# A two-layer decoder trunk on one core: the first expert pair in two halves, a norm's rows by transfer, gathers that skip empty slots, and buffers handed to the weight stream in another order

## The chip, the cores and the metric

The kernel runs on one core of a Trainium2 chip. Its time is device microseconds of one execution. The engines are TensorE (PE; its weight loads are listed apart as PEld), VectorE (DVE), ScalarE (ACT), GpSimd (POOL) and SyncE (SP). SP computes nothing here: it issues the weight transfers one after the other. ACT and POOL issue transfers too.

## The reference, cut to what matters

256 tokens of 1024 features go through two layers. Each layer mixes tokens (layer A by a gated linear recurrence, layer B by stick-breaking attention, both with four heads of attention into a fixed memory), projects the result, adds it to the input and normalises; then a mixture of experts follows, with a second add and norm.

```python
x = post_norm(x, mixed @ w_o[layer], ln_mix_g[layer], ln_mix_b[layer])
moe_out = hier_moe(x, w_group[layer], b_group[layer], w_router[layer], b_router[layer],
                   w_gate[layer], w_up[layer], w_down[layer])
x = post_norm(x, moe_out, ln_ffn_g[layer], ln_ffn_b[layer])
...
# hier_moe: top-1 of 4 groups, then top-2 of its 4 experts; 16 experts of 256 inner features
h = jax.nn.silu(jnp.einsum('td,edf->tef', xf, w_gate)) * jnp.einsum('td,edf->tef', xf, w_up)
y = jnp.einsum('tef,efd->td', h * gates[:, :, None].astype(h.dtype), w_down)
```

## The kernel before, in words

**Experts by pairs.** Each token goes to 2 of 16 experts. An expert has 64 slots (`CAP`), and two experts make a pair of 128 slots, one per partition. So there are 8 pairs, 1024 slots, and 512 of them hold a token when none overflows; the rest are empty. In `Moe.run` a pair p goes through these steps: `gu` multiplies its 128 rows by the gate and up weights (8 blocks `kk` of 128 features, two experts `c` side by side in two column halves of PE, 512 output columns: 256 of gate, 256 of up); ACT takes silu of the gate half and DVE multiplies by the up half and the slot's weight (`h`, lines 873 and 875); PE transposes `h` (`ht`, line 899), ACT copies it to `hT` (line 900), PE multiplies by the down weights (`po`, line 913) in two halves of 512 columns. A matmul of the program on float32 shows as two records in the trace. In pairs 1 to 7, blocks of the next pair's `gu` stand between these steps, so that PE has work while ACT and DVE finish. Pair 0 has no such work in between: `gu(0)`, `turn(1)` (two small matmuls `ptp`), two `ht`, then `po`. Pair 0's `h` is already cut into two column halves for ACT and DVE, but both halves of gate and up lie in one PSUM bank, and all of `gu(0)` ends first.

**Rows of a pair.** Pair 0's rows are made by matmuls with a one-hot matrix. For pairs 1 to 7 the normalised tokens `z` are stored to a buffer `zd` in HBM and gathered into one of two row tiles `zg` (POOL, `fetch`, line 673) by an index per slot; PE then transposes the rows (`xgp`, line 791), and ACT and DVE apply the norm's gain and bias per feature. The index of an empty slot is 256, and a gather leaves out indices above 255. `zg` is not cleared, so for pairs 1 and 2, the first ones into each tile, line 665 takes the index down to at most 255: their empty slots fetch row 255. The later gathers leave empty slots out. Output rows of pairs 0 to 4 are scattered to a buffer `hd` (line 760) and brought back per token near the end (line 752); pairs 5 to 7 are combined by matmuls into `y`.

**The weight stream.** All weights are 133 chunks of 1 MB in the order of use. `Stream` issues them on SP, in a fixed order, and at most three are under way (`DEPTH`: a chunk is issued when the third before it has landed). A chunk goes to a free buffer: nine in a ring `w`, and other tiles that are free for a while (`x0`, `x1`, `m0`, `m1`, `wa` to `wd`, `o0`, `gb`), which `stream.open` hands over. `late` chunks, the first two of each layer's experts, go to the tiles `u` and `ex` by `stream.send`. Each pair takes six chunks: two for `kk` 0 to 3 (one per expert), two for `kk` 4 to 7, two for `po`. Layer A's experts are chunks 23 to 70, layer B's 85 to 132. A chunk that waits for its buffer holds back every chunk behind it on SP.

**Norm rows.** `rows` brings gain and bias of a norm into the tile `gb`: one row by transfer, and two broadcasts over the partitions on POOL (line 384); for the last norm the transfer itself writes all 128 partitions (line 380). `affine` applies them to the tokens on DVE (lines 438 and 440), token half 0 after `gu(0)`, half 1 behind pair 0's `h`. Then `gb` is opened for weights.

**Order.** Inside the two mixer ends DVE, PE and ACT keep the written order, and so does what `pin` marks; the rest is placed by a scheduler that simulates the program. So the changed source does not by itself tell the order of instructions.

Of the kernel before, what the change touches and what calls it, by code (L numbers as in the profile page):

```python
# [15 lines left out]
P = 128  # L16
D = 1024
# [25 lines left out]
def trunk(ctx: ExitStack, tc: tile.TileContext, w_all, x_tok_d, cst_d, msk_d, rw_d, rb_d,  # L43
# [331 lines left out]

    def rows(which, name, by_transfer=False):

        gb = tok_tile("gb", f"gb{name}")
        if by_transfer:
            nc.scalar.dma_start(gb, ln_d[0, 2 * which:2 * which + 2].partition_broadcast(P))  # L380
            return gb
        nc.scalar.dma_start(gb[0:1], ln_d[:, 2 * which:2 * which + 2])
        for v in range(2):
            ins = nc.gpsimd.partition_broadcast(gb[:, v], gb[0:1, v])  # L384
            if which % 2:
                tc.keep_in_program_order(ins)
        return gb

    class Norm:
# [39 lines left out]
        def apply(self, dst, src):  # L429
            nc.scalar.activation(dst, src, AF.Identity, scale=self.r, bias=self.nmr)  # L430

# [111 lines left out]
    class Moe:  # L543
# [87 lines left out]
        def start(self, pool):  # L631
            self.work = pool
            self.zg = slots.tile([P, 2, D], F32, tag="o1", name=f"zg{self.l}")

        def gather_first(self, z, t):

            l = self.l
            P0 = self.P0[:, t].rearrange("p e c -> p (e c)")
            if t == 0:
                self.first = [bank(f"xgp{l}", tag="y", shape=(P, 4, P)) for _ in range(2)]  # L640
            for hk in range(2):
                for k in range(4):
                    kk = 4 * hk + k
                    nc.tensor.matmul(self.first[hk][:, k], z[:, t, kk * P:(kk + 1) * P], P0, start=(t == 0 and k == 0),
                                     stop=(t == 1 and k == 3), skip_group_check=True)
# [7 lines left out]
        def indices(self):  # L653

            l = self.l
            self.P1f = self.P1.rearrange("p t e c -> p t (e c)")
            self.idx = self.rt("idx", (8,), I32)
            ps = bank(f"idx{l}", tag="m", shape=(P, 8))
            for p in range(8):
                for t in range(NT):  # L660
                    nc.tensor.matmul(ps[:, p:p + 1], self.P1f[:, t, p * P:(p + 1) * P], tokb[:, t:t + 1], start=(t == 0),
                                     stop=(t == 1))


            pin(nc.vector.tensor_scalar(self.idx[:, 0:3], ps[:, 0:3], float(T), T - 1.0, op0=ALU.add, op1=ALU.min))
            for p in (1, 2):
                self.fetch(p)
            self.filled = self.rt("filled", (8,))
            nc.vector.tensor_scalar(self.idx[:, 3:8], ps[:, 3:8], float(T), None, op0=ALU.add)
            nc.vector.tensor_copy(self.filled, ps)  # L670
# [132 lines left out]
        def run(self, xg):  # L803
# [7 lines left out]

            def gu(p, ks):

                if p not in ws:
                    ws[p] = [stream.get() for _ in range(6)]
                    gus[p] = bank(f"gu{l}", tag="y" if p <= AWAY else "m")
                for kk in ks:
                    kh, k = kk // 4, kk % 4
                    for c in range(2):
                        pin(nc.tensor.matmul(gus[p][c * 64:(c + 1) * 64], xgs[p][:, kk, c * CAP:(c + 1) * CAP],  # L820
                                            ws[p][2 * kh + c][0][:, k * 512:(k + 1) * 512], start=(kk == 0),
                                            stop=(kk == NK - 1)))
                    if k == 3:
                        stream.done(ws[p][2 * kh][1], ws[p][2 * kh + 1][1])
# [11 lines left out]
            for p in range(8):  # L836
                if p == 0:
                    gu(0, range(4))
                    self.gates()
                    self.turn(0)  # L840
                    gu(0, range(4, 8))
                    self.ex = slots.tile([P, 2, D], F32, tag="ex", name=f"ex{l}")
# [28 lines left out]
                parts = [slice(0, 256)] if p else [slice(0, P), slice(P, 256)]  # L871
                for c in parts:
                    nc.scalar.activation(h[:, c], gus[p][:, c], AF.Silu)  # L873
                for c in parts:
                    pin(nc.vector.scalar_tensor_tensor(h[:, c], gus[p][:, 256 + c.start:256 + c.stop],
                                                       self.gsl[:, p:p + 1], h[:, c], op0=ALU.mult, op1=ALU.mult))
                if p == 0:
# [14 lines left out]
                if p == 7:  # L892
                    beyond(pool, self.pool, self.ex, l, base, self.x1, self.most, self.late, y)
                hT = pool.tile([P, 2, P], F32, name=f"hT{l}")
                for c in parts:
                    fs = slice(c.start // P, c.stop // P)
                    ht = bank(f"ht{l}", tag="m", shape=(P, 2, P))
                    for f in range(fs.start, fs.stop):
                        pin(nc.tensor.transpose(ht[:, f], h[:, f * P:(f + 1) * P], ident))  # L899
                    nc.scalar.activation(hT[:, fs], ht[:, fs], AF.Copy)  # L900
                if 0 < p < 7:
                    gu(p + 1, range(2, 3))
# [5 lines left out]
                for hf, s in enumerate(half if p < 7 else quarters):  # L908
                    n = s.stop - s.start
                    po = bank(f"po{l}", tag="m")[:, 0:n]  # L910
                    for f in range(2):
                        for c in range(2):
                            pin(nc.tensor.matmul(po[c * 64:(c + 1) * 64], hT[:, f, c * 64:(c + 1) * 64],  # L913
                                                ws[p][4 + c][0][:, f * D + s.start:f * D + s.stop],
                                                start=(f == 0), stop=(f == 1)))
                    if p >= AWAY:
# [19 lines left out]

    def mixer_end(op, res, l, lasts, fill, finish):

# [21 lines left out]
        def z(t):  # L960
            norms[t].apply(s[:, t], s[:, t])
            return (nc.scalar, nc.gpsimd if l == 0 else nc.scalar)[t].dma_start(moe.zd[t * P:(t + 1) * P], s[:, t])

# [106 lines left out]
        xg = moe.first_rows()  # L1070
        gb = rows(2 * l, f"m{l}")
        for p in moe.run(xg):
# [3 lines left out]
            if p is None:  # L1076
                affine(x1, s, gb, ts=(1,))
                stream.open(("gb",), end - 12, keep)
            if p == 6 + l:
                gb = rows(2 * l + 1, f"o{l}", l == 1)  # L1080
        tags[0] = "my"
# [376 lines left out]
    with tc.tile_pool(name="sbp", bufs=1, reuse_waits="tile") as sbp:  # L1458
# [87 lines left out]
        with tc.tile_pool(name="attb", bufs=1, reuse_waits="tile") as pool:  # L1546
# [5 lines left out]
            run(fl)  # L1552
    stream.open(("x0", "x1"), EXPERTS_END[1])
    wparts.use("wa", "wb", "wc", "wd")
# [4 lines left out]
    def heads():  # L1559
        for hp in range(6):  # L1560
            po = bank("so", shape=(P, T))
            with together() as add:
                for j, own in enumerate((slice(0, T), slice(P, T))):
                    for c in (1, 0):
                        h = 2 * hp + c
                        add(nc.tensor.matmul(po[c * 64:(c + 1) * 64, own], vB[:, j, h * 64:(h + 1) * 64],
                                             at_head(h)[:, 256 * j:256 + 128 * j], start=(j == 0), stop=(j == 1)))
            put_mixed(mixed, hp, po)
            yield
    fl = op.main(range(2))  # L1570
    next(fl)
    weave(heads(), fl, 0.5)
    run(fl)
    stream.send(EXPERTS_END[1] - 48, keep, "u")
    stream.send(EXPERTS_END[1] - 47, slots, "ex")
    for q in (2, 3):
        for h in range(2):
            op.weights(q, h)
    stream.open(("m0", "m1"), EXPERTS_END[1])

    def into_output(moe, work, add, norms, s, o, gb):
# [10 lines left out]
        with tc.manual_schedule(engines={mybir.EngineType.DVE}):  # L1592
# [17 lines left out]
            bias(1, 1)  # L1610
    mixer_end(op, x2, 1, [2, 3], iter(()), into_output)

# [89 lines left out]
```

## Time and profile before

| | |
|---|---|
| three runs | 527.27, 530.89, 527.27 us; median 527.27 |
| the profiled execution | 526.96 us, of which its span is 525.3 us |
| PE busy | 491.1 us, 93% of the span |
| DVE, ACT, POOL busy | 300.2, 229.6, 62.9 us |
| transfers | 161.61 MB, mean 308 GB/s over the span |

The page gives busy time by engine, the span in 40 slices, and groups of instructions. The other views order the same trace by time, by wait, or by stretch. Times are from the start of the span, in us. Layer A's experts run from 166 to 278, layer B's from 409 to 513.

### The profile page before, as it was taken

What the parts mean: (1) busy time and instruction counts of PE and PEld (TensorE: products, weight loads), DVE (VectorE), ACT (ScalarE), POOL (GpSimd) and SP (SyncE); (2) the same over time, 40 slices, a digit from 0 to 9 for tenths busy, and PEclk for the clock granted to TensorE, in tenths of its full rate; (3) what the DMA queues carried; (4) which work ended last, traced back from release to release, by engine and by line L of the source; (5) the groups of instructions that cost most, each with busy time, mean ns of one, the idle gap of its engine ahead of it and who ended that gap; (6) DMA issues with size and microseconds to landing.
All of it is one profiled execution on the core that took longest, in us unless ns stands there. A gap on an engine that the chain in (4) does not pass through costs nothing. (4 is left out here: it accounts for less than half of the span.)

```text
span 525.3 us, 9096 instructions
## 1 busy us (share of the span) xinstructions
PE 491.1 (93%) x3534; PEld 326.7 (62%) x3534; DVE 300.2 (57%) x682; ACT 229.6 (44%) x471; POOL 62.9 (12%) x78
## 2 busy tenths in 40 slices
PE   4999999999999999999797999998998899999992
PEld 4998898788996333333236889877687333333431
DVE  4668876867758622233338698677445842233547
ACT  4845446684445222333017566668423232222322
POOL 1100000002132111112011500000010121111201
PEclk9999999999999999999898999999998999999997
DMA  8999834447888999999999763242999799999922
GB/s 270 407 404 404 345 103 160 161 156 326 299 332 321 384 403 384 394 385 407 409 379 395 271 252 143 100 160 99 381 365 364 288 382 419 414 422 409 412 119 81
DMA packets 28439, 161.61 MB, mean 308 GB/s; under 512 B 5239, under 2 KB 5623, under 8 KB 11363
## 3 DMA queue, kind: packets, MB, share of 16 engines
q1 hardware_dynamic: 20736, 140.76, 68.3%
q0 software_dynamic: 4752, 10.94, 5.4%
q10 hardware_dynamic: 2902, 9.26, 4.8%
q8 instruction: 30, 0.49, 0.4%
q14 instruction: 19, 0.16, 0.1%
HBM read 158.92 MB, written 13.64 MB: 329 GB/s over the span
## 5 line engine op out<-in xcount | busy, mean ns | idle before, releaser
L820 PE MATMUL gu<-w,ex 128*64 128x512 f32 x256 | 62.9, 609 | 3.4 <-DMA w<-in_w_all_dram 2.3
L820 PE MATMUL gu<-w,xg 128*64 128x512 f32 x256 | 60.8, 601 | 0.1
L913 PE MATMUL po<-w,hT 128*64 128x512 f32 (+1 forms) x272 | 58.4, 570 | 0.1
L913 PEld LDWEIGHTS po<-w,hT 128*64 128x64 f32 x272 | 18.8, 136 | 34.0 <-issue 27.3
L820 PEld LDWEIGHTS gu<-w,ex 128*64 128x64 f32 x256 | 17.2, 137 | 34.8 <-issue 26.1
L820 PEld LDWEIGHTS gu<-w,xg 128*64 128x64 f32 x256 | 16.4, 136 | 26.5 <-issue 24.6
L920 DVE COPY hr<-po 128x512 f32<-128x512 f32 x10 | 6.9, 692 | 43.1 <-PE po L913 43.0
L629 ACT ACTIVATE xg<-xgp,lnT 128x128 f32<-128x128 f32 x32 | 13.5, 457 | 25.6 <-PE xgp L791 22.4
L918 DVE TENSOR_TENSOR hl<-po,hl 128x512 fp32r<-128x512 f32 (+1 forms) x14 | 8.5, 615 | 26.5 <-ACT hl L917 25.5
L627 DVE TENSOR_SCALAR xg<-xgp,lnT 128x128 f32<-128x128 f32 x32 | 12.4, 408 | 19.0 <-ACT xg L629 15.7
L629 ACT ACTIVATE ex<-xgp,lnT 128x128 f32<-128x128 f32 x32 | 14.3, 458 | 19.3 <-PE xgp L791 19.0
L627 DVE TENSOR_SCALAR ex<-xgp,lnT 128x128 f32<-128x128 f32 x32 | 13.1, 410 | 15.1 <-ACT ex L629 13.9
L900 ACT ACTIVATE hT<-ht 128x256 f32<-128x256 f32 (+1 forms) x18 | 6.5, 360 | 34.4 <-PE ht L899 34.3
L873 ACT ACTIVATE h<-gu 128x256 f32<-128x256 f32 (+1 forms) x18 | 6.3, 360 | 34.3 <-PE gu L820 34.3
L234 DVE TENSOR_TENSOR wo<-w,wo 128x512 fp32r<-128x512 f32 x20 | 13.7, 727 | 10.8 <-ACT wo L226 10.8
L760 POOL DMA_INDIRECT hd<-hr,own x10 | 10.1, 1014 | 81.2 <-DVE gsl L780 76.3
L673 POOL DMA_INDIRECT zg<-zd,idx x14 | 14.6, 1041 | 43.2 <-PE xgp L791 25.1
L791 PEld LDWEIGHTS xgp<-cst,zg 128*128 128x128 f32 x112 | 12.0, 141 | 11.4 <-PE gu L820 7.3
L1291 POOL TENSOR_TENSOR rms<-rms,neghalf 128x2 f32<-128x2 f32 x6 | 4.1, 699 | 111.6 <-ACT sq L1287 99.4
L384 POOL PARTITION_BROADCAST gbm<-gbm x4 | 5.3, 1398 | 94.2 <-DMA gbm<-in_ln_dram 85.5
L226 ACT ACTIVATE wo<-w 128x512 fp32r<-128x512 f32 x20 | 11.5, 628 | 9.8 <-PE wo L472 8.2
L917 ACT ACTIVATE hl<-po 128x512 fp32r<-128x512 f32 (+1 forms) x14 | 7.5, 537 | 18.4 <-PE po L913 18.4
(462 smaller groups left out, 1357.7 us busy)
## 6 DMA issues: line engine op xcount, KB each, us to landing
w<-in_w_all_dram SPq DMA_DIRECT2D x131, 1024.0 KB
hd<-in_w_all_dram ACTq DMA_DIRECT2D x2, 2560.0 KB
w<-in_w_all_dram SPq DMA_DIRECT2D x6, 256.0 KB
x_tok<-in_x_tok_dram ACTq DMA_DIRECT2D x1, 1024.0 KB
zd<-z ACTq DMA_DIRECT2D x2, 512.0 KB
gbo<-in_ln_dram ACTq DMA_DIRECT2D x1, 1024.0 KB
out_dram<-z SPq DMA_DIRECT2D x4, 256.0 KB
w<-in_w_all_dram SPq DMA_DIRECT2D x1, 512.0 KB
```

The source lines that it names most:

```text
L226: self.last_hi = nc.scalar.activation(p[:, 0, s], src[:, s], AF.Copy, scale=1.0 if scale is None else scale).ins
L234: nc.vector.tensor_sub(p[:, 1, s], src[:, s], p[:, 0, s])
L627: ins = nc.vector.tensor_scalar(xg[:, kk], ps, g, b, op0=ALU.mult, op1=ALU.add)
L629: nc.scalar.activation(xg[:, kk], ps, AF.Identity, scale=g, bias=b)
L673: nc.gpsimd.indirect_dma_start(out=self.zg[:, p % 2], out_offset=None, in_=self.zd, in_offset=bass.IndirectOffsetOnAxis(ap=self.idx[:, p:p ...
L760: pin(nc.gpsimd.indirect_dma_start(out=self.hd, out_offset=bass.IndirectOffsetOnAxis(ap=self.own[:, p:p + 1], axis=0), in_=src, in_offset= ...
L791: pin(nc.tensor.transpose(ps[:, k], self.zg[:, p % 2, (4 * hk + k) * P:(4 * hk + k + 1) * P], ident))
L820: pin(nc.tensor.matmul(gus[p][c * 64:(c + 1) * 64], xgs[p][:, kk, c * CAP:(c + 1) * CAP], ws[p][2 * kh + c][0][:, k * 512:(k + 1) * 512], ...
L913: pin(nc.tensor.matmul(po[c * 64:(c + 1) * 64], hT[:, f, c * 64:(c + 1) * 64], ws[p][4 + c][0][:, f * D + s.start:f * D + s.stop], start=( ...
L917: self.hl_last = nc.scalar.activation(hl[:, 0, s], po, AF.Copy).ins
L918: pin(nc.vector.tensor_sub(hl[:, 1, s], po, hl[:, 0, s]))
L920: nc.vector.tensor_copy(hr[:, p % 2, s], po)
```

## The change

Five edits, the last two in the layer B half of the program.

1. **Pair 0 in halves.** `gu(0)` is cut into two halves j of 256 columns, each 128 of gate and 128 of up, each in a PSUM bank of its own. `kk` 0 to 3 run both halves; `kk` 4 to 7 run all of half 0, then all of half 1. `po` is cut too (`down`): the products with inner features 0 to 127 (f=0) for both output halves stand between the two `ht`, the others (f=1) behind.
2. **Gathers.** Line 665's limit to 255 goes; instead ACT fills both `zg` tiles with zeros once, behind the last use of `z` (layer A) or the second store of it (layer B).
3. **Layer B's mixer norm.** Its rows come by one transfer over all partitions into the slot `x1`, issued on ACT before the output projection, instead of one row and two broadcasts into `gb`.
4. **Buffers of layer B.** `gb` is opened to the stream before the experts, `x1` only behind the affine; `ex` is sent earlier; `m0` and `m1` are opened one by one while the attention heads finish.
5. **The last norm's rows** are requested behind the last `hl` copy of pair 6, where the scheduler had put them at pair 4.

```diff
@@ class Moe
             self.zg = slots.tile([P, 2, D], F32, tag="o1", name=f"zg{self.l}")
+            with tc.issue_after(self.last_z.ins):
+                for i in range(2):
+                    nc.scalar.activation(self.zg[:, i], zrow[:, 0:1].to_broadcast([P, D]), AF.Copy)
...
-            pin(nc.vector.tensor_scalar(self.idx[:, 0:3], ps[:, 0:3], float(T), T - 1.0, op0=ALU.add, op1=ALU.min))
+            pin(nc.vector.tensor_scalar(self.idx, ps, float(T), None, op0=ALU.add))
             for p in (1, 2):
                 self.fetch(p)
             self.filled = self.rt("filled", (8,))
-            nc.vector.tensor_scalar(self.idx[:, 3:8], ps[:, 3:8], float(T), None, op0=ALU.add)
             nc.vector.tensor_copy(self.filled, ps)
...
-            def gu(p, ks):
+            def gu(p, ks, parts=(0, 1)):
...
-                    gus[p] = bank(f"gu{l}", tag="y" if p <= AWAY else "m")
+                    gus[p] = [bank(f"gu{l}", tag="y" if p <= AWAY else "m") for _ in range(1 if p else 2)]
                 for kk in ks:
                     kh, k = kk // 4, kk % 4
...
+                    for j in range(1) if p else parts:
+                        for c in range(2):
+                            w = ws[p][2 * kh + c][0][:, k * 512:(k + 1) * 512]
+                            if p == 0:
+                                w = w.rearrange("p (g h n) -> p h g n", g=2, h=2)[:, j]
+                            out = gus[p][j][c * 64:(c + 1) * 64]
+                            pin(nc.tensor.matmul(out if p else out[:, 0:256], xgs[p][:, kk, c * CAP:(c + 1) * CAP], w,
+                                                start=(kk == 0), stop=(kk == NK - 1)))
...
                     gu(0, range(4))
                     self.gates()
                     self.turn(0)
-                    gu(0, range(4, 8))
+                    for j in range(2):
+                        gu(0, range(4, 8), (j,))
...
+                def down(po, s, fs):
+                    for f in fs:
+                        for c in range(2):
+                            pin(nc.tensor.matmul(po[c * 64:(c + 1) * 64], hT[:, f, c * 64:(c + 1) * 64],
+                                                ws[p][4 + c][0][:, f * D + s.start:f * D + s.stop],
+                                                start=(f == 0), stop=(f == 1)))
+                pos = [bank(f"po{l}", tag="m") for _ in half] if p == 0 else []
                 for c in parts:
...
                     nc.scalar.activation(hT[:, fs], ht[:, fs], AF.Copy)
+                    if p == 0 and fs.start == 0:
+                        for po, s in zip(pos, half):
+                            down(po, s, (0,))
@@ def mixer_end
-        gb = rows(2 * l, f"m{l}")
+        gb = rows(0, "m0") if l == 0 else gb1
...
-                stream.open(("gb",), end - 12, keep)
+                stream.open(*((("gb",), end - 12, keep), (("x1",), end))[l])
             if p == 6 + l:
-                gb = rows(2 * l + 1, f"o{l}", l == 1)
+                if l == 0:
+                    gb = rows(1, "o0")
+                else:
+                    with tc.issue_after(moe.hl_last):
+                        gb = rows(3, "o1", True)
@@ layer B, around the output projection
-    stream.open(("x0", "x1"), EXPERTS_END[1])
+    gb1 = rows(2, "m1", True, slots.tile([P, NT, D], F32, tag="x1", name="gbm1"))
+    stream.send(EXPERTS_END[1] - 47, slots, "ex")
+    stream.open(("x0",), EXPERTS_END[1])
...
+            if hp in (2, 4):
+                stream.open((f"m{hp // 2 - 1}",), EXPERTS_END[1])
...
+    stream.open(("gb",), EXPERTS_END[1] - 12, keep)
     stream.send(EXPERTS_END[1] - 48, keep, "u")
-    stream.send(EXPERTS_END[1] - 47, slots, "ex")
...
-    stream.open(("m0", "m1"), EXPERTS_END[1])
```

How the order moves. First PE in pair 0 of layer A, from the end of `gu(0)` (layer B reads alike). Before:

```order
L773 MATMUL ptp0_2209<-G30_2168,P10_1866 128x48
L899 MATMUL ht0_2220<-cst_87,h0_2204 128x128
L899 MATMUL ht0_2223<-cst_87,h0_2204 128x128
L913 MATMUL po0_2226<-w27_1515,hT0_2219 64x512
L913 MATMUL po0_2226<-w28_1536,hT0_2219 64x512
L913 MATMUL po0_2226<-w27_1515,hT0_2219 64x512
L913 MATMUL po0_2226<-w28_1536,hT0_2219 64x512
L791 MATMUL xgp0_2232<-cst_87,zg0_2105 128x128 x4
L791 MATMUL xgp0_2241<-cst_87,zg0_2105 128x128 x4
```

Both `ht` stand together, and all four products of the first output half behind them. In the change (here the numbers of the buffers are left out, and `gu(0)` of half 1 stands ahead of the first row):

```order
L775 MATMUL ptp_2227<-G_2178,P_1866 128x48
L915 MATMUL ht_2240<-cst,h_2222 128x128
L907 MATMUL po_2238<-w_1515,hT_2237 64x512
L907 MATMUL po_2238<-w_1536,hT_2237 64x512
L907 MATMUL po_2239<-w_1515,hT_2237 64x512
L907 MATMUL po_2239<-w_1536,hT_2237 64x512
L915 MATMUL ht_2247<-cst,h_2222 128x128
L907 MATMUL po_2238<-w_1515,hT_2237 64x512
L907 MATMUL po_2238<-w_1536,hT_2237 64x512
L793 MATMUL xgp_2253<-cst,zg_2105 128x128 x4
L793 MATMUL xgp_2262<-cst,zg_2105 128x128 x4
```

The second `ht` moved behind four products, and two products follow it at once.

Then SP in layer B, where chunks 102 to 110 are issued (`w107` is chunk 107). Before:

```order
L94 DMA w102_4240<-in_w_all_dram 128x2048
L94 DMA w105_4394<-in_w_all_dram 128x2048
L94 DMA w106_4396<-in_w_all_dram 128x2048
L94 DMA w107_4414<-in_w_all_dram 128x2048
L94 DMA w108_4464<-in_w_all_dram 128x2048
L94 DMA w109_4466<-in_w_all_dram 128x2048
```

And in the change:

```order
L94 DMA w102_4260<-in_w_all_dram 128x2048
L94 DMA w107_4448<-in_w_all_dram 128x2048
L94 DMA w105_4428<-in_w_all_dram 128x2048
L94 DMA w106_4430<-in_w_all_dram 128x2048
L94 DMA w108_4498<-in_w_all_dram 128x2048
L94 DMA w110_4511<-in_w_all_dram 128x2048
```

Chunk 107 moved ahead of 105 and 106. Its buffer was `gb` and is now `x1`; either holds the norm's rows until the affine of token half 1 has read them.

## Rows read from the trace of the kernel before

**Rows 1.** The page, busy time by engine.

```profile
PE 491.1 (93%) x3534; PEld 326.7 (62%) x3534; DVE 300.2 (57%) x682; ACT 229.6 (44%) x471; POOL 62.9 (12%) x78
```

**Rows 2.** Waits by engine, PE alone: waiter, releaser, total us, times, longest.

```profile
PE ht L899 <- DVE h L875: 1.6, 2, 0.8
```

**Rows 3.** Timeline of PE, layer A, pair 7: start, us, instruction, idle before.

```profile
248.91 1.46 PE L820 MATMUL gu<-w,xg 128*64 128x512 f32 x6
251.45 1.04 PE L820 MATMUL gu<-w,ex 128*64 128x512 f32 x2 [1.08 <-DVE h L875]
254.79 3.57 PE L820 MATMUL gu<-w,ex 128*64 128x512 f32 x6 [2.30 <-DMA w<-in_w_all_dram]
```

**Rows 4.** Stretches: length, busy us of PE, PEld, DVE, ACT, POOL; clock, DMA share, GB/s.

```profile
254.94:258.34 3.40, 3.40 (x7) 0.56 (x5) 1.97 (x2) 0.00 (x0) 0.00 (x0) 0.50 1.02 418
509.00:512.80 3.80, 3.80 (x26) 1.71 (x25) 1.06 (x2) 0.98 (x2) 0.00 (x0) 1.00 0.02 4
```

**Rows 5.** Timeline of SP, layer A, weight transfers in a row, and one alone.

```profile
176.77 78.37 SPq L94 DMA_DIRECT2D w<-in_w_all_dram  x27
...
254.81 0.33 SPq L94 DMA_DIRECT2D w<-in_w_all_dram  x1
```

**Rows 6.** A stretch of layer A's experts, columns as in Rows 4.

```profile
236.00:250.00 14.00, 14.00 (x76) 4.96 (x72) 5.79 (x14) 4.54 (x11) 2.99 (x3) 1.00 0.99 402
```

**Rows 7.** Transfers by queue, 165 to 181: packets, MB, share of 16 engines.

```profile
q0 software_dynamic: 291, 1.05, 16.4%
```

**Rows 8.** The same view, 432.9 to 437: pair 4's gather in layer B alone.

```profile
q0 software_dynamic: 157, 0.29, 18.4%
```

**Rows 9.** Timeline of PE, layer A, pair 0.

```profile
173.91 0.22 PE L773 MATMUL ptp<-G,P 128*128 128x48 bf16 x2
174.93 0.65 PE L899 MATMUL ht<-cst,h 128*128 128x128 f32 x2 [0.80 <-DVE h L875]
175.62 1.94 PE L913 MATMUL po<-w,hT 128*64 128x512 f32 x8
...
178.51 1.94 PE L913 MATMUL po<-w,hT 128*64 128x512 f32 x8
180.28 1.03 PE L820 MATMUL gu<-w,ex 128*64 128x512 f32 x4
```

**Rows 10.** Timeline of PE, layer B, pair 7's down products, x8 of 512, x16 of 256.

```profile
509.13 3.66 PE L913 MATMUL po<-w,hT 128*64 128x512 f32 x24
```

**Rows 11.** Timeline of ACT, end of layer A's mixer.

```profile
158.96 1.24 ACT L430 ACTIVATE x_tok<-x_tok,normx 128x1024 f32<-128x1024 f32 x1 [0.97 <-DVE normx L427]
160.22 1.28 ACT L699 ACT_TABLE_LOAD   x1
162.68 0.21 ACT L699 ACTIVATE ex<-ex 128x10 f32<-128x10 f32 x1 [1.17 <-DVE ex L694]
...
166.07 1.51 ACT L629 ACTIVATE xg<-xgp,lnT 128x128 f32<-128x128 f32 x4 [1.40 <-PE xgp L644]
```

**Rows 12.** Timeline of ACT, layer B: its first work behind the second store's issue.

```profile
406.67 0.21 ACT L699 ACTIVATE ex<-ex 128x10 f32<-128x10 f32 x1 [3.89 <-DVE ex L694]
```

**Rows 13.** Waits of SP's queue.

```profile
SPq L94 <- DVE x L440: 3.1, 1, 3.1
```

**Rows 14.** Timelines of SP and PE, layer B: chunks 105 to 131; 131 alone; pair 7's start.

```profile
416.85 75.67 SPq L94 DMA_DIRECT2D w<-in_w_all_dram  x27
...
492.20 0.33 SPq L94 DMA_DIRECT2D w<-in_w_all_dram  x1
...
493.06 1.46 PE L820 MATMUL gu<-w,ex 128*64 128x512 f32 x6
```

**Rows 15.** Transfers by queue, 465 to 472: the last norm's rows.

```profile
q10 hardware_dynamic: 144, 1.05, 35.8%
```

**Rows 16.** Timeline of ACT, the copy behind which edit 5 asks; chain, norm's gain.

```profile
502.12 0.60 ACT L917 ACTIVATE hl<-po 128x512 fp32r<-128x512 f32 x1 [1.12 <-PE po L913]
...
516.52 0.74 DVE w L1586
```

More of the change, by code (lines that the diff above doesn't have):

```diff
@@ L374, in tok_tile, with rows @@
         return keep.tile([P, NT, D], F32, tag=which, name=name)
-    def rows(which, name, by_transfer=False):
-        gb = tok_tile("gb", f"gb{name}")
+    def rows(which, name, by_transfer=False, gb=None):
+        gb = tok_tile("gb", f"gb{name}") if gb is None else gb
         if by_transfer:
@@ L429, in apply @@
         def apply(self, dst, src):
-            nc.scalar.activation(dst, src, AF.Identity, scale=self.r, bias=self.nmr)
+            return nc.scalar.activation(dst, src, AF.Identity, scale=self.r, bias=self.nmr)
     def affine(dst, z, gb, norms=None, ts=range(NT)):
@@ L810, in run @@
             quarters = [slice(0, 512), slice(512, 768), slice(768, D)]
-            def gu(p, ks):
+            def gu(p, ks, parts=(0, 1)):
                 if p not in ws:
                     ws[p] = [stream.get() for _ in range(6)]
-                    gus[p] = bank(f"gu{l}", tag="y" if p <= AWAY else "m")
+                    gus[p] = [bank(f"gu{l}", tag="y" if p <= AWAY else "m") for _ in range(1 if p else 2)]
                 for kk in ks:
                     kh, k = kk // 4, kk % 4
[L819 to L823, printed above, removed]
+                    for j in range(1) if p else parts:
[6 more added lines that the diff above has]
+                                                start=(kk == 0), stop=(kk == NK - 1)))
+                    if k == 3 and 1 in parts:
                         stream.done(ws[p][2 * kh][1], ws[p][2 * kh + 1][1])
@@ L871, in run @@
                 parts = [slice(0, 256)] if p else [slice(0, P), slice(P, 256)]
[L872 to L876, printed above, removed]
+                n = 256 // len(parts)
+                for c, got in zip(parts, gus[p]):
+                    nc.scalar.activation(h[:, c], got[:, 0:n], AF.Silu)
+                for c, got in zip(parts, gus[p]):
+                    pin(nc.vector.scalar_tensor_tensor(h[:, c], got[:, n:2 * n], self.gsl[:, p:p + 1], h[:, c],
+                                                       op0=ALU.mult, op1=ALU.mult))
                 if p == 0:
@@ L909, in run @@
                     n = s.stop - s.start
[L910 to L915, printed above, removed]
+                    po = pos[hf] if p == 0 else bank(f"po{l}", tag="m")[:, 0:n]
+                    down(po, s, (1,) if p == 0 else range(2))
                     if p >= AWAY:
@@ L934, in run, with mixer_end @@
             self.y = y
-    def mixer_end(op, res, l, lasts, fill, finish):
+    def mixer_end(op, res, l, lasts, fill, finish, gb1=None):
         tags[0] = "m"
@@ L960, in z @@
         def z(t):
-            norms[t].apply(s[:, t], s[:, t])
-            return (nc.scalar, nc.gpsimd if l == 0 else nc.scalar)[t].dma_start(moe.zd[t * P:(t + 1) * P], s[:, t])
+            moe.last_z = norms[t].apply(s[:, t], s[:, t])
+            store = (nc.scalar, nc.gpsimd if l == 0 else nc.scalar)[t].dma_start(moe.zd[t * P:(t + 1) * P], s[:, t])
+            if l == 1:
+                moe.last_z = store
+            return store
         def more(n):
@@ L1610, in into_output @@
             bias(1, 1)
-    mixer_end(op, x2, 1, [2, 3], iter(()), into_output)
+    mixer_end(op, x2, 1, [2, 3], iter(()), into_output, gb1)
 _INS = ["w_all", "x_tok", "cst", "msk", "rw", "rb", "lnT", "ln", "lowT"]
```

## The prediction, made before the changed kernel ran

> **What bounds the kernel now.** I read the busy times first. PE is at work for 491.1 us, 93% of the span, and DVE, next, for 57% [rows 1]. So a change gains where PE idles, or where its clock is low. The waits of PE then say where that is, and the timelines what stands at each place.
>
> Three places bear on this change. The first is pair 0 of each layer: its `ht` waits 0.8 us for DVE's `h`, once per layer [rows 2]. The second is layer A's pair 7. Six records of `gu` start at 248.91, the next two at 251.45 after 1.08 idle, the next six at 254.79 after 2.30 idle, released by a weight transfer [rows 3]. In layer B the same first six records start at 493.06 and take 1.46 too, and PE has no such wait there [rows 14]. Six records take 1.46 and two 1.04 with the gaps' lead-in, so some 3.9 us are lost in layer A: 251.45 is 1.1 to 1.25 late, and 254.79 is 2.3 to 2.65 late behind it. The third follows at once: from 254.94 to 258.34 the granted clock is 0.50, that is 1.2 GHz, though PE is busy throughout [rows 4]. It does in 3.4 us what 1.7 would do at full clock; what it did before was to idle.
>
> Why does layer A's weight stream come late? SP issues 27 chunks from 176.77 on, the last of them, shown alone, at 254.81 [rows 5]: 26 intervals in 78.0 us, 3.00 us a chunk. In the middle of this the transfer engines are 0.99 busy and move 402 GB/s [rows 6]. The stream here is limited by transfers, and everything else moved on the same engines delays it. A chunk is issued when the third before it has landed, so the issue at 254.81 dates the landing of the chunk that PE resumes on at 254.79.
>
> **Gathers without empty slots.** Between 165 and 181 the gathers of pairs 1 and 2 move 1.05 MB, 256 rows of 4 KB, at 16.4% of 16 us, which is 2.62 us of all 16 engines [rows 7]. The limit in line 665 makes each empty slot fetch a row. Without it only filled slots fetch: 512 of 1024 slots are filled, half on the average, and pair 4 in layer B, which already skips, moves 0.29 MB, 71 rows of 128 [rows 8]. Half of 1.05 MB goes, 0.524 MB. At 402 GB/s [rows 6] this is 1.30 us, at the queue's own share half of 2.62 = 1.31. It comes before the chunk that PE waits for in pair 7, the stream is full in between, so PE resumes 1.3 us earlier: **−1.3**. Bounds: 0, if a skipped slot costs as much as a fetched one; the nearest row against that is pair 4, 18.4% of 4.1 us = 0.75 us for 71 rows, against 1.31 for 128 [rows 7, 8], so the price goes with the rows. The other end is 71 of 128 rows, 57 saved per pair, 0.467 MB or 1.16 us, to 1.5 us if these two pairs are emptier.
>
> A rule stands against the rate. The Trainium skill, "DMA: Bandwidth & Descriptors", Specifications, gives about 358 GB/s for HBM to one core; by it, an estimate, 0.524 MB would be worth 1.46 us. The row's 402 GB/s lies above that figure, so the measurement decides, and the sum keeps 1.30.
>
> In layer B the same bytes go, but no wait on weights stands at pair 7 [rows 14], so there the gain is room, not time.
>
> The **zero fill** is two ACT passes over 128x1024; the nearest row of that shape took 1.24 [rows 11], so 2.5 us per layer. In layer A ACT is done with its token work at 158.96 + 1.24 = 160.20. Then the fill would run to 162.7 and the table load of 1.28 to 164.0, so `ex`, at 162.68 before, goes 1.3 later. The next work that `gu(0)` needs, the copies to `xg` at 166.07, had ACT idle for 1.40 [rows 11]; that takes in the 1.3. In layer B the fill follows the second store, where ACT idles 3.89 until 406.67 [rows 12]. The gathers, which must now stand behind the fill, start after 165 in layer A, later than it ends. Cost 0 in both; if that cover failed, `xg` and with it `gu(0)` would slip, by at most 2.5 us per layer.
>
> **Pair 0 in halves.** Before, from the end of `gu(0)` (`ptp`, 173.91) to `gu(1)` (180.28) 6.37 us pass [rows 9]. The bubbles in it are the 0.80 before `ht`, and what is left of the copy to `hT` behind it, some 0.35: 1.15 in all. In the change half 0 of `gu` ends about 1.75 us before half 1 (16 of the new records), and `h` took about 1.0 from 173.91 to 174.93, so `ht` of half 0 can run at +0.2, behind `ptp`. Before, the first product started 0.69 behind the first `ht` (174.93 to 175.62) [rows 9]; so `po` at about +0.9, eight records of f=0 at 1.77 (178.51 to 180.28 is eight) to +2.65, then `ht` of half 1, whose `h` is ready by then. But nothing stands between this `ht` and its products: a second bubble, again up to 0.69, to +3.3; then eight records at 1.77 and `xgp` at 1.02 between them: +6.15, against 6.37: −0.2. Against it, `gu(0)` is issued as 64 records of 256 columns instead of 32 of 512. The only rows of that width are in pair 7: 24 records in 3.66 less overlap, some 3.59 until the next instruction [rows 10]; take off eight wide ones at 0.221 = 1.77, and 16 narrow ones take 1.82, 0.114 each against 0.111 for half a wide one. 64 × 0.003 = 0.2 at most, 0.1 taken. Net **−0.1** per layer, between +0.2 (the split costs, the bubbles stay) and −1.15 (both go).
>
> In layer A this is no gain at all: PE comes 0.1 earlier to a chunk that lands when transfers allow. It counts in layer B alone.
>
> **Layer B's norm rows.** A transfer of 1.05 MB replaces two broadcasts on POOL, which does not bound (12%) [rows 1]. It is asked for over 30 us before affine needs it. Cost 0; one broadcast transfer of this size took 35.8% of 7 us = 2.5 us of the engines [rows 15], which lengthens the queue of weights there, but PE does not wait for weights in that stretch.
>
> **Buffers of layer B.** SP waits 3.1 us for DVE's affine at line 440 [rows 13], for chunk 107; chunks 105 and 106 were issued ahead of this, from 416.85 [rows 14]. In the change 107 comes first, so 105 and 106 stand behind the wait, and go at 416.85 + 3.1 + issue, 420.6 to 420.8: 3.8 to 4.0 later. On the other side the last norm's rows no longer go among the weights: their 2.5 us of transfers [rows 15] are asked for behind the copy at 502.12 [rows 16] and are needed at 516.52, 14 us later, so hidden. What is left is 3.9 − 2.5, about 0.7 to 1.5 us later for the chunks of pair 7. The issue of chunk 131 at 492.20 dates the landing of chunk 128, and PE starts on pair 7's weights at 493.06 with its first chunk, the second 0.43 later [rows 14]: slack 0.9 to 1.3. With the gathers' 1.3 on top as room, PE does not wait. Cost 0, and this is the least certain term.
>
> **The sum**, against the profiled execution's 526.96: −1.3 (layer A) − 0.1 (layer B) = 525.6. The median of the runs shown is 527.27, 0.3 above the profiled one. 1%, about what a measurement of this kernel can tell from no change, is 5.3 us; so this is no change.
>
> **The rivals.**
> *The clock's fall goes too* (18%). The low clock behind layer A's wait followed 3.4 us of idling in two pieces [rows 3, 4]; with 1.3 less it may not come. For it: layer B has waits under 1 us in this place and no fall. Against it: 2.1 us of idling remain. Gain 1.7 more: 523.9.
> *The buffer order starves layer B's pair 7* (12%), the other side. SP stands behind affine 3.1 us, and 105 and 106 go 4.0 later. If the stream has no slack between 420 and 490, as in layer A, and the room from the last norm's rows comes too late or not at all, chunk 128 lands 4.0 later, beyond 1.3 of slack: PE waits 2.7, and the clock falls as in layer A, 1.7 more. 526.96 − 1.4 + 2.7 + 1.7 = 530.0. It decides from the point where chunk 128 lands over 1.3 later. For it: such an order of waits; against it: 2.5 us of transfers taken from just that stretch.
> *Two banks cost the clock* (3%). If the alternation between two banks in pair 0 made the clock fall there, 1.7 each layer [rows 4] would be added, the layer A part on top of the wait moved: about 525.6 + 3.4 = 529.0. Against it, pair 7's products cross banks from 509.0 to 512.8 at granted clock 1.00 [rows 4]. The Trainium skill, "TensorE: Matmul & The Clock Gate", "A second HAM failure mode: psum-queue depth-cycling", tells of a clock that swings where PE goes through banks with short idles between groups; that stretch, which has no idles, doesn't show it.
> *Skipped slots cost as fetched ones* (10%), so the gathers do not change what the stream has: 526.9.
> *Both of pair 0's bubbles go* (5%): 1.15 instead of 0.1 in layer B: 524.5.
> My forecast has 52%.
>
> **The numbers.** The likeliest is 525.6. The range reaches down over the clock's case, 523.9, with 1.15 of pair 0's bound on it, 522.8, and up over the two-bank case and most of the buffer one, 529.5. Of both sides little is left out. Faster by over 1% would be 522.0 or less: the clock's case, both bubbles and an emptier pair together, 9%. Slower by over 1%, 532.6 or more: the starving of pair 7 with more than one chunk late, 4%. Within 1%: 87%.
>
> **What would show it.** In layer A's pair 7, PE's last late group starts at about 253.5 instead of 254.79, behind a transfer still; queue q0 moves about 0.5 MB from 165 to 181; the clock of the 3.4 us behind it is 0.50 (or 1.00, the first rival). In pair 0, `ht` follows `ptp` at once, and two gaps of about 0.3 to 0.4 stand before the products; `gu(1)` starts 6.15 after `gu(0)` ended. In layer B, SP waits about 3 us on line 440's successor and 105 is issued near 420.7; pair 7 shows no wait for a transfer, and the last norm's rows land before 516. The prediction is wrong if PE restarts in layer A at 254.8, if it waits for a weight in layer B, or if ACT's zero fill delays the `ex` of the routing.

## The result, and the profile after

The changed kernel took 522.56 us in the median of 20 runs, the kernel before 526.64 in 20 runs beside it; the ratio is 0.9944, interval 0.9921 to 0.9966, 3 us less (1.8 to 4.2). The ratio leaves out executions in a slower state of the chip; the medians, over all of them, differ by 4.1 us. The profiled execution took 522.80 (span 521.1). The forecast, no change beyond 1%, held. By the ratio the forecast's 526.96 becomes 524.0, inside its range of 522.8 to 529.5; the median of 522.56 itself lies 0.2 below that range. The reasons given did not hold.

PE, layer A, pair 7, in the changed kernel: start, us, instruction, idle before (answers to [rows 3]).

```profile
247.48 2.80 PE L827 MATMUL gu<-w,xg 128*64 128x512 f32 x12
250.10 1.89 PE L827 MATMUL gu<-w,ex 128*64 128x512 f32 x8
...
267.26 0.41 PE L915 MATMUL ht<-cst,h 128*128 128x128 f32 x2 [2.79 <-DVEq L489]
267.42 1.61 PE L834 MATMUL y<-hl,PT 128*128 128x512 f32 x4
268.96 4.84 PE L907 MATMUL po<-w,hT 128*64 128x512 f32 x24
```

No wait for weights is left, where 1.3 us less of it was forecast. But `ht` now waits 2.79 us for DVE, and `po` behind it takes 4.84 us instead of 3.66 (layer B before, [rows 10]), at a granted clock of 0.75 from 268.96 to 273.73. DVE, then POOL, say why; the last DVE row is the same pass in layer B:

```profile
262.44 2.12 DVE L802 TENSOR_TENSOR zg<-zg,second 128x1024 f32<-128x1024 f32 x1 [1.92 <-DMA zg<-hd,back]
264.60 2.07 DVE L803 SCALAR_TENSOR_TENSOR zg<-x,zg 128x1024 f32<-128x1024 f32 x1
266.58 0.47 DVE L883 SCALAR_TENSOR_TENSOR h<-gu,gsl,h 128x256 f32<-128x256 f32 x1
...
500.73 1.23 DVE L802 TENSOR_TENSOR zg<-zg,second 128x1024 f32<-128x1024 f32 x1 [2.68 <-DMA zg<-hd,back]
```

```profile
262.32 3.40 POOL L384 PARTITION_BROADCAST gbo<-gbo  x2 [10.07 <-issue]
```

`join` (lines 802, 803) stands ahead of pair 7's `h` on DVE. It adds the output rows that were brought back per token, so it waits for a gather, and beside POOL's broadcast its passes take 2.1 us instead of 1.23. Pair 0 and its queue of gathers (answers to [rows 7, 9]):

```profile
173.94 0.22 PE L775 MATMUL ptp<-G,P 128*128 128x48 bf16 x2
174.01 0.31 PE L915 MATMUL ht<-cst,h 128*128 128x128 f32 x1
174.68 1.94 PE L907 MATMUL po<-w,hT 128*64 128x512 f32 x8 [0.37 <-ACT hT L916]
176.55 0.33 PE L915 MATMUL ht<-cst,h 128*128 128x128 f32 x1
177.24 1.08 PE L907 MATMUL po<-w,hT 128*64 128x512 f32 x4 [0.37 <-ACT hT L916]
...
180.19 1.03 PE L827 MATMUL gu<-w,ex 128*64 128x512 f32 x4
```

```profile
q0 software_dynamic: 288, 0.43, 7.4%
```

The prediction had put another place at no cost. POOL, layer B's mixer end, in the kernel before and then in the changed one; line 410 is the norm's power, which follows DVE's line 409:

```profile
383.01 2.48 POOL L384 PARTITION_BROADCAST gbm<-gbm  x2 [85.50 <-DMA gbm<-in_ln_dram]
396.10 0.59 POOL L410 TENSOR_TENSOR normx<-normx,neghalf 128x1 f32<-128x1 f32 x1 [10.61 <-issue]
```

```profile
392.31 0.55 POOL L410 TENSOR_TENSOR normx<-normx,neghalf 128x1 f32<-128x1 f32 x1 [97.39 <-DVE normx L409]
```

Before, the power starts 10.61 us after the broadcast ended, and nothing that the profile calls work lies between; DVE's line 409 had started at 394.66, 1.44 us earlier. After, the power waits for DVE alone and starts 0.23 behind line 409 (392.08). What DVE does next, line 413, needs the power, again before and then after:

```profile
396.73 0.16 DVE L413 TENSOR_TENSOR normx<-normx 128x1 f32<-128x1 f32 x1 [1.91 <-POOL normx L410]
```

```profile
392.90 0.16 DVE L413 TENSOR_TENSOR normx<-normx 128x1 f32<-128x1 f32 x1 [0.66 <-POOL normx L410]
```

The order of POOL in the kernel before had this to read, before the run:

```
114 L384 ISA
115 L384 ISA gbm_4341<-gbm_4341 128x1024 x2
116 L410 ISA
117 L410 TENSOR_TENSOR normx_4103<-normx_4103,neghalf 128x1
```

Where the bare ISA rows stand, at 114 and 116, the trace has MODIFY_POOL_CONFIG: two at line 384, and two at line 410 at the broadcast's end, six in all behind the three pairs of broadcasts (line 410 in the kernel before: count, ns, first and last start):

```profile
L410 POOLq MODIFY_POOL_CONFIG  x6: 127/127/127, 147.7 to 385.4; - x6
```

They take 0.13 us each. I read the idle time behind them as POOL's set-up for the other kind of work; the trace itself shows the two records and the time in which nothing runs. In the change the broadcast is gone, and both rows with it.

### The profile page after: what moved, and what is told of

The parts are those of the page before. It is cut to its first block, busy times and chain, and to the rows that moved or that the text cites. A ratio compares the mean times of both kernels' runs of the same rounds, so it can differ in the third digit from the quotient of the medians.

```text
span 521.1 us, 9217 instructions
## 1 busy us (share of the span) xinstructions
PE 486.9 (93%) x3598; PEld 329.6 (63%) x3598; DVE 301.2 (58%) x680; ACT 233.6 (45%) x475; POOL 62.2 (12%) x76
## 5 line engine op out<-in xcount | busy, mean ns | idle before, releaser
L907 PE MATMUL po<-w,hT 128*64 128x512 f32 (+1 forms) x272 | 60.0, 580 | 1.5 <-ACT hT L916 1.5
L827 PE MATMUL gu<-w,xg 128*64 128x512 f32 (+1 forms) x320 | 60.9, 514 | 0.1
L827 PE MATMUL gu<-w,ex 128*64 128x512 f32 x256 | 60.2, 598 | 0.0
L827 PEld LDWEIGHTS gu<-w,xg 128*64 128x64 f32 x320 | 21.0, 136 | 23.7 <-issue 18.3
L793 PE MATMUL xgp<-cst,zg 128*128 128x128 f32 x112 | 15.3, 280 | 0.0
L937 ACT ACTIVATE hr<-po 128x512 f32<-128x512 f32 x10 | 6.0, 597 | 20.7 <-PE po L907 20.7
```

The lines of the kernel that those rows point to most:

```text
L793: pin(nc.tensor.transpose(ps[:, k], self.zg[:, p % 2, (4 * hk + k) * P:(4 * hk + k + 1) * P], ident))
L827: pin(nc.tensor.matmul(out if p else out[:, 0:256], xgs[p][:, kk, c * CAP:(c + 1) * CAP], w, start=(kk == 0), stop=(kk == NK - 1)))
```

## The experiments

Each ratio is to the kernel before, run beside it on the same chip. The runs were made in three sets on three chips: e1 to e4; x1, x2, x4 and j1; y1, y2, b1 and j3. The changed kernel itself was run in none of them.

A stretch of each kernel is compared: from layer B's first `wo` product of the output projection to `slot` of token half 0, and from there to `gu(0)`. Columns as in [rows 4]. Of the kernel before, then the changed one:

```profile
367.57:398.97 31.40, 30.92 (x175) 24.34 (x173) 14.56 (x36) 11.50 (x23) 3.07 (x3) 1.00 0.94 378
398.97:409.44 10.47, 8.14 (x66) 7.52 (x66) 7.86 (x34) 3.19 (x7) 0.56 (x1) 0.84 0.92 345
```

```profile
364.99:395.75 30.76, 30.76 (x174) 24.29 (x173) 14.70 (x36) 11.52 (x23) 0.55 (x1) 1.00 0.99 398
395.75:404.14 8.39, 6.47 (x68) 5.88 (x67) 7.41 (x34) 5.09 (x9) 0.55 (x1) 1.00 1.00 385
```

Together 41.87 us before, 39.15 after. `slot` is the product that counts tokens into slots, and it hangs on the norm's power; so a late power lengthens the first part, and a low clock behind it the second.

**e1_gather**, the kernel before with edit 2.

```diff
+ zero fill of zg;  - limit to T - 1 on idx[:, 0:3]
```

> The kernel before with the gather edit alone (zero fill, no limit on the index). Theory: the 0.6 MB that the first gathers no longer move in layer A end PE's wait for the weight chunks of pair 7 (3.9 us) and the low clock behind it (1.7 us), and 2 to 3 of these 5.6 us are given back behind it, where pair 7's ht waits for DVE's join of the last rows brought back. So 2 to 3.5 us faster than before, the whole gain of the change. In its trace no wait for a weight in layer A's pair 7, and an ht wait of about 2.8 us there. Rival: the gain of the change comes from layer B (edits 3 to 5, the clock's fall at 402 us that is gone); then this is 1.3 us faster or less.

Ratio 0.9993 (0.9961 to 1.0025): nothing, so the rival. Its trace, of its longest run (530.73, median 526.91), has no wait for a weight in layer A's pair 7, as expected, and loses more than that in layer B: this stretch took 46.73 us, PE waited for `slot`, and the clock was at its lower level almost to `gu(0)`. Waits of PE, the two stretches, and POOL:

```profile
PE slot L605 <- DVE Ab L597: 2.9, 1, 2.9
```

```profile
365.08:398.87 33.79, 30.92 (x175) 24.34 (x173) 14.97 (x36) 11.51 (x23) 3.46 (x3) 0.98 0.94 374
398.87:411.81 12.94, 11.03 (x66) 10.27 (x66) 8.28 (x35) 4.56 (x7) 0.55 (x1) 0.52 0.62 232
```

```profile
381.19 2.87 POOL L384 PARTITION_BROADCAST gbm<-gbm  x2 [86.15 <-DMA gbm<-in_ln_dram]
396.00 0.59 POOL L410 TENSOR_TENSOR normx<-normx,neghalf 128x1 f32<-128x1 f32 x1 [11.94 <-issue]
```

**e2_limit**, the changed kernel without edit 2.

```diff
- zero fill of zg;  + limit to T - 1 on idx[:, 0:3]
```

> The changed kernel with the gather edit undone (limit to 255 back, no zero fill), all else as changed. Theory: PE's wait in layer A's pair 7 is back, over 2 us, so the time is within 1 us of the kernel before (526.6). Rival (gain from layer B's edits): it stays near the changed kernel, 523 to 524.

0.9945 (0.9907 to 0.9982): by the ratio the rival (523.7 from 526.6), though its times spread from 520.93 to 535.62, with a median of 525.62. No wait in layer A, though the limit is back; 3.8 us of waiting for weights in layer B's pair 7.

**e3_halves**, the kernel before with `gu`, `down` and `pos` of edit 1.

```diff
- gu(0, range(4, 8))
+ for j in range(2): gu(0, range(4, 8), (j,))
```

> The kernel before with pair 0 in halves alone. Theory: 0.1 us less in layer B, nothing in layer A, where PE then waits for the weight chunk of pair 7 as before: no difference, within 0.5 us. Rival (both bubbles of pair 0 go): 1.15 us faster or more.

1.0027 (0.9988 to 1.0066): nothing, as expected. But its trace has no wait for weights in layer A's pair 7, which the theory took to stay. The layer B stretch: 46.03 us, with the low clock.

**e4_buffers**, the kernel before with edits 3 to 5.

```diff
+ gb1 = rows(2, "m1", True, ...);  + stream.open / send in the new places;  + rows(3, "o1", True) behind hl_last
```

> The kernel before with edits 3 to 5 alone (norm rows of layer B by transfer, buffers and order of layer B, last norm's rows later). Theory: no difference, within 0.7 us; chunk 128 lands 1 to 1.5 us nearer to its use, without a wait. Rival: the clock's fall at 402 us in layer B's mixer end and 0.9 us ahead of it go with these edits, 2.5 us faster. Other rival: layer B's pair 7 now waits for a weight, 2 us slower or more.

0.9885 (0.9836 to 0.9934): the whole gain, and more than the first rival's 2.5 us. Its mechanism came in half: the first part of the stretch is as short as in the change, but the clock still falls once in the second.

```profile
362.33:393.10 30.77, 30.77 (x175) 24.30 (x173) 14.70 (x36) 11.52 (x23) 0.55 (x1) 1.00 0.98 399
393.10:403.11 10.01, 8.10 (x68) 7.50 (x67) 7.40 (x34) 3.19 (x7) 0.55 (x1) 0.83 0.98 373
```

40.78 us together. No broadcast stands there, so such a fall is not POOL's alone (j1_join has it too). The theory of the gathers fell, and the next one was POOL.

**x1_rows**, the kernel before with edit 3's transfer. It goes into `gb`, not `x1`, and so later than in the change: it is issued 13.3 us behind the stretch's first `wo` product, and in the change (and in e4) 1.9 us ahead of it.

```diff
- gb = rows(2 * l, f"m{l}")
+ gb = rows(2 * l, f"m{l}", l == 1)
```

> The kernel before with one argument changed: layer B's mixer norm rows come by one transfer into the same tile gb, so POOL broadcasts nothing there. New theory: behind its broadcast POOL reconfigures (two MODIFY_POOL_CONFIG at line 410) and starts its next tensor operation, the norm's power at line 410, only 8 to 12 us after the broadcast ended; DVE, then PE, wait for that power, and the clock falls behind the wait. Without the broadcast the power follows DVE's line 409 within 0.3 us, PE's wait for slot (2.2 and 2.9 us in the kernels without edit 3) is 0, the 33 us from the first wo product to slot become 30.8, and the stretch from slot to gu(0) 8.4 to 10 us instead of 13. 3 to 6 us faster, the whole gain of the change. Rival: the gain comes from the buffers' order (edit 4); then this stays within 1 us of before.

The mechanism came, the time did not: 0.9991 (0.9948 to 1.0033), where the rival had it. Its trace is of its longest run (536.61, median 529.10): in layer A POOL's power came 11.98 us behind the broadcast, and `gu(0)` 9 us late. The stretch in layer B is as the theory has it:

```profile
373.87:404.63 30.76, 30.76 (x175) 24.28 (x173) 14.34 (x36) 11.40 (x23) 0.55 (x1) 1.00 0.95 382
404.63:413.01 8.38, 6.46 (x67) 5.87 (x66) 7.40 (x34) 3.19 (x7) 0.55 (x1) 1.00 1.01 380
```

```profile
PE gu L820 <- DMA w<-in_w_all_dram: 3.1, 2, 2.6
```

39.14 us, and behind it PE waits for layer B's weights. The other runs fit this. The time that a low clock costs, (1 − clock) × span, is 7.9 us in the median of the runs that count for the ratio, and 10.6 in the kernel before beside it. So 2.7 us less go to the clock, in the same time, and as much is lost elsewhere.

**x2_early**, the changed kernel with the broadcast back, early.

```diff
- gb1 = rows(2, "m1", True, slots.tile(...))
+ gb1 = rows(2, "m1", False, slots.tile(...))
```

> The changed kernel, but the rows of layer B's mixer norm again by one row and two POOL broadcasts, now where the change asks for them, some 17 us earlier than in the kernel before. Theory: the reconfiguration runs from about 370 to 380 us, ends before DVE's line 409 (about 392), and costs nothing: as fast as the changed kernel, within 1 us. Rival: the broadcast itself (it shares something with DVE, or lies late) is the price wherever it stands: 2 us slower or more than the changed kernel.

521.98 us, 0.9878 (0.984 to 0.9917): no slower than the change, with 0.9944 beside its own kernel before. The broadcast itself costs nothing here, 23 us ahead of line 409; what cost time in this stretch was where it stood.

```profile
365.98 2.83 POOL L384 PARTITION_BROADCAST gbm<-gbm  x2 [71.99 <-DVE mixB L367]
392.07 0.60 POOL L410 TENSOR_TENSOR normx<-normx,neghalf 128x1 f32<-128x1 f32 x1 [23.25 <-DVE normx L409]
```

```profile
364.73:395.50 30.77, 30.77 (x175) 24.31 (x173) 14.70 (x36) 11.52 (x23) 3.43 (x3) 1.00 0.97 394
395.50:403.88 8.38, 6.47 (x68) 5.87 (x67) 7.39 (x34) 5.08 (x9) 0.56 (x1) 1.00 0.96 335
```

**x4_late**, the changed kernel with a small broadcast.

```diff
+ with tc.issue_after(added.ins): pin(nc.gpsimd.partition_broadcast(dum, zrow[0:1]))
```

> The changed kernel with one small broadcast more on POOL (8 columns, read by nothing), behind DVE's first add of layer B's mixer end, some 8 us before line 409. Theory: it alone brings the wait back: the power at line 410 starts 8 to 12 us after that broadcast, PE waits 1 to 4 us for slot, the clock falls behind it; 2 to 7 us slower than the changed kernel. Rival (bytes or time of the big broadcast count, not the reconfiguration): no difference.

522.27 us, 0.987 (0.9822 to 0.9918): inconclusive. The broadcast ran at 305.88 and not behind the add, so it only says once more that an early one is free. That a late one alone brings the wait back was not shown.

**j1_join**, the changed kernel with `join`'s passes exchanged.

```diff
- zg = zg + other;               zg = ALPHA * x1 + zg
+ other = ALPHA * x1 + other;    zg = zg + other
```

> The changed kernel with join's two passes exchanged: alpha times x1 is added to the second rows first, and the gathered rows are added last, so one DVE pass instead of two stands between the landing of the last gather and pair 7's h. Theory: the wait of ht in pair 7 (2.8 us in layer A, 1.8 in layer B) falls by 1.2 in each layer, the low clock behind it in layer A may go: 2 to 4 us faster than the changed kernel. Rival: the wait is set by the gather's landing alone, or later work swallows it: within 1 us.

520.06 us, 0.9833 (0.9791 to 0.9875), the lowest. The intervals of x2_early and x4_late, run beside it, overlap with its own, so its lead on the change is not shown by time. In its trace the waits of `ht` are lower than the changed kernel's 2.79 and 1.78:

```profile
PE ht L915 <- DVEq L489: 1.0, 1, 1.0
PE ht L915 <- PEq L489: 0.3, 1, 0.3
```

But x2_early, without the exchange, has much the same, and x4_late 0.8 and 1.0, so that the edit lowered them is not shown either. x2_early:

```profile
PE ht L915 <- DVEq L489: 1.4, 1, 1.4
PE ht L915 <- PEq L489: 0.3, 1, 0.3
```

**y1_late_rows** is x1_rows with edit 5, **y2_rows_gather** x1_rows with edit 2. The norm rows' transfer is as late in both as in x1_rows.

```diff
+ with tc.issue_after(moe.hl_last): gb = rows(3, "o1", True)     (y1)
+ zero fill of zg;  - limit to T - 1 on idx[:, 0:3]              (y2)
```

> The kernel before with two parts of the change: layer B's mixer norm rows by transfer (into gb, as x1_rows) and edit 5, the last norm's rows asked for behind pair 6's last hl copy. Theory: x1_rows won its 4 to 6 us in layer B's mixer end and lost 3.1 us plus 1.5 us of clock to a wait for weights in layer B's pair 7; 1 MB less in that stretch (2.5 us of the engines) takes most of this wait away. So 3 to 5 us faster than before, and a wait for weights in layer B's pair 7 of at most 0.7 us. Rival: the buffers' order (edit 4) gives the room; then it stays within 1 us of before.

> The kernel before with two other parts: layer B's mixer norm rows by transfer (into gb) and the gather edit. Theory: the gathers' 0.6 MB less in layer B (1.4 us of the engines) take away about half of x1_rows's wait in pair 7: 1.5 to 3.5 us faster than before, a wait for weights of 1 to 2 us there. Rival: the gathers do nothing (as alone, e1_gather): within 1 us of before.

Both missed: 1.001 (0.9974 to 1.0047) and 1.0111 (1.0044 to 1.0178), the second slower than the kernel before. The stretch took 39.15 and 39.14 us. y2's trace waits for weights in pair 7; y1's has no such wait, but it is of that kernel's shortest run (521.61, median 525.72). Of y2:

```profile
PE gu L822 <- DMA w<-in_w_all_dram: 4.4, 2, 2.4
```

**b1_nobcast** is j1_join with both norms' rows of layer A by transfer, **j3_both** with the last norm's alone.

```diff
- gb = rows(0, "m0") / gb = rows(1, "o0")
+ gb = rows(0, "m0", True) (b1) / gb = rows(1, "o0", True) (both)
```

> j1_join with layer A's norm rows by transfer too, both of them, so that POOL broadcasts nowhere. Theory: in layer A's mixer end DVE no longer waits 3.3 us for the power behind POOL's reconfiguration, gu(0) of layer A starts 2.5 to 3 us earlier, and join runs at its undisturbed 1.2 us a pass: 2 to 4 us faster than j1_join (which was 6 to 8 faster than before). Rival: the stream of layer A, with 1 MB more ahead of pair 7 and PE 2.7 us earlier, makes pair 7 wait 1 to 4 us and the clock fall there: no gain on j1_join, or up to 3 us slower.

> j1_join with the last norm's rows of layer A alone by transfer (no broadcast beside join). Theory: join's passes in layer A take 1.2 us instead of 2.1, ht's wait in pair 7 falls from 1.0 to 0.3: 0.5 to 1 us faster than j1_join. Rival: the transfer delays the last gather by 1 us or more, and nothing is won.

0.9996 (0.9949 to 1.0042) and 1.0022 (0.9978 to 1.0065): no gain on the kernel before is left. j1 was not run beside them, so a difference of the chips is not ruled out. In b1's layer A DVE waits 0.66 for the power instead of the 3.25 in the kernel before, which is the mechanism again; but `gu(0)` starts at 166.68, no earlier than the 166.58 there: line 409 came 1.2 later, and of the 2.6 us less waiting 1.1 reached `gu(0)`. PE waits for weights in both layers; j3 waits in layer B. Of b1, then j3:

```profile
PE gu L827 <- DMA w<-in_w_all_dram: 6.3, 3, 3.4
```

```profile
PE gu L827 <- DMA w<-in_w_all_dram: 3.8, 2, 2.6
```

## Why the prediction was right, and where its reasons failed

No change was right, the sum behind it was not: −1.4 was forecast and −3.0 (−1.8 to −4.2) measured. A gain that was counted was not there, and one that was counted as nothing was; both were under 1%. So that the forecast held owes something to luck. By stages the two profiled executions differ like this, in us:

| from | to | before | after |
|---|---|---|---|
| start | layer A's `gu(0)` | 166.58 | 166.58 |
| `gu(0)` | `gu(1)` | 13.70 | 13.61 |
| `gu(1)` | layer B's first product | 105.51 | 103.01 |
| there | the first `wo` product | 81.78 | 81.79 |
| there | layer B's `gu(0)` (the stretch) | 41.87 | 39.15 |
| `gu(0)` | `gu(1)` | 13.70 | 13.61 |
| `gu(1)` | end | 102.15 | 103.38 |

**The gathers, −1.3: failed.** The bytes went as forecast (0.43 MB instead of 1.05; 0.52 was taken). But the step read one execution's wait in layer A as the kernel's. Of 14 traces, three have it: the kernel before, x4_late and b1_nobcast, the last two with the gather edit; e2, e3, e4, x1 and y1 have the limit and no wait. What x4_late adds to the changed kernel runs in layer B alone (at 305.88), and yet it waits in layer A, where the changed kernel did not:

```profile
254.22 3.24 PE L827 MATMUL gu<-w,ex 128*64 128x512 f32 x6 [2.16 <-DMA w<-in_w_all_dram]
```

From SP's issue at 172.96 in the kernel before to that at 251.38, 26 chunks later, the three took 78.4 to 79.4 us, all others 74.2 to 77.5. So these transfers run up to 7% faster or slower from one trace to the next, 5 us here, more than the 1.3 that the edit saves. The 2.5 us of layer A in the table are such a draw, one execution's and not the edit's: the kernel before waited and the changed one did not, and `ht` gave part of it back.

**"A transfer replaces two broadcasts on POOL, which does not bound. Cost 0": failed, and this stage's gain is there.** POOL is 12% busy, but the time behind its MODIFY_POOL_CONFIG is not busy in the profile. The broadcast's end to the power: 10.61, 11.94 and 11.11 us in the three traces with the late broadcast (before, e1, e3). DVE waited 1.9, 4.3 and 3.6 us for the power, and 0.7 in the others; PE's `slot` waited 0.5, 2.9 and 2.2; and the low clock behind that cost more. The stretch took 41.87, 46.73 and 46.03 us there, 39.14 to 40.78 in the eleven others. The other runs say the same by their mean granted clock: its median is 0.980 in the runs of the kernel before that count, on each of the three chips, and 0.987 in those of the change. (1 − clock) × span is 10.5 us against 6.7, so by this estimate 3.8 us less is lost to the clock, about the 3 us gained.

The Trainium skill, "GPSIMD Engine Reference", Instruction dispatch, says that the first call of a freshly loaded POOL kernel pays about 6 us that show as no instruction. The trace agrees that nothing is shown; it has 8 to 12 us here. By the page's figure the set-up would, as an estimate, have ended at 391.5, ahead of DVE's 394.66, and cost nothing; the measured 10.6 decides.

**Pair 0, −0.1 per layer: right.** From `gu(0)` to `gu(1)` 13.70 us became 13.61 in both layers; the two bubbles are 0.37 each, as forecast.

**Zero fill, 0: right.** Its two passes took 1.99 us, not 2.5, and `ex` went 0.73 later (163.41 after 162.68), not 1.3. The prediction calls a later `ex` both expected and a sign of being wrong; what decides is that in layer A `xg` starts at 166.07 in both kernels.

**Buffers, 0 with 4.0 us later issues: right for the changed kernel, with less room than thought.** Chunk 105 went 4.0 later against `gu(0)` and PE did not wait. In other executions it does: e2, b1 and j3, of eight traces with edit 4, and x1 and y2, of six without. From SP's issue at 416.85 in the kernel before to that at 489.08, 25 chunks later, the traces that wait 1 us or more there took 73.0 to 76.0 us, those that don't 68.6 to 72.2, or had their mixer end late (e1, 74.4). So the rival's wait is real, and with its low clock it costs what edit 3 won in x1 and y2. That the order of edit 4 makes it is not shown, since kernels without that order wait too.

**Where the total came from, then.** In the pair of traces 2.7 us come from layer B's stretch, 2.5 from the draw in layer A, 0.2 from pair 0, and 1.2 are given back behind layer B's `gu(1)`, where `ht` waits 1.78 instead of 0.30 for `join`. Of the two large terms the stretch alone is shown as the edits' doing: x1 and x2 give its cause, and the clock of the other runs goes with it. That this becomes time is another matter. Edits 3 to 5 gain together (e4), and 3 alone or 3 with 5 do not (x1, y1), which points to edit 4's order of buffers. But x1 and y1 also ask for the norm rows some 15 us later than e4 does. Edit 4 alone, and edit 3 at the change's own place without edit 4, were not run. And e2, b1 and j3 have all of edits 3 to 5 and wait, the three sets were on three chips, and one trace each doesn't tell a kernel's stream from an execution's. So the cause of the total stays open.

## What to carry to other kernels

Before an operation on a lightly used engine is costed at nothing, look in its order for what stands between it and the next operation there: two kinds of work on POOL in turn cost 8 to 12 us of set-up here, which needs to be early or to be avoided. A wait that one profile shows for a saturated stream can be a draw; take its size from several executions, or bound it from zero. And a wait removed ahead of a stream that is just in time can come back as a wait for the stream.

## What the runs showed of the hardware

- POOL's tensor operation behind a partition broadcast, with two MODIFY_POOL_CONFIG between, started 7.8 to 8.4 us after the broadcast ended in layer A's mixer end (once 11.98, in x1), and 10.6 to 11.9 in layer B's. Meanwhile the transfer engines were 0.83 to 0.89 busy in the first (before, after, e1, e3, x1) and fully busy, 0.99 or more, in the second (before, e1, e3); that this is the reason is not shown.
- With the broadcast 23 us ahead (x2), the tensor operation started as soon as DVE had its input ready.
- `join`'s DVE passes of 1.23 us took up to 2.17 beside a POOL broadcast (x2), and a broadcast of 1.30 took up to 2.40 beside such a pass (e4).
